# Output stage of a two-layer hybrid backbone: low halves and second gate factor to VectorE, retention rows and gate row loaded from GpSimd's queue

## The chip, the cores and the metric

The kernel runs on one core of one Trainium2 chip. Its metric is the device time in microseconds (us) of one execution. Before the change it was 3836.28 us, the median of three runs (3832.0 to 3844.18).

## The reference

Two layers are applied to a stream of 2048 latent tokens and 256 context tokens, each 1024 wide. One input projection feeds three groups of heads: latent attention (8 heads, 512 columns), retention (4 heads, 256 columns) and a convolution module (256 columns). Every group is multiplied by its own SiLU gate, the groups are joined, sent through one output projection, gated and normalised:

```
o_mla  = softmax(q k^T * scale) v  *  silu(pg_mla)
o_ret  = norm(retention forward + backward) * silu(pg_ret)
o_conv = conv_module(pglu) * silu(pg_conv)
y      = concat([o_mla, o_ret, o_conv]) @ w_out          # 1024 x 1024
x_new  = layer_norm(ALPHA * x + gate * y, ln_g, ln_b)
```

The context rows are needed in the first layer only; the second layer (`l == 1`, "layer 1" below) returns the 2048 latent rows.

## The kernel before, in words

Tokens are handled in units of 256 columns and tiles of 128 tokens (two tiles to a unit). Each layer has three stages: input projections, attention, output. The diff lies in the class `Output`, which does the last one. Its first generators already run beside the last quarter of attention's last head.

**What one unit needs.** `gen_prep` makes the left operand of the output projection. SyncE (its DMA queue is SP) loads the attention rows and the convolution rows of a unit into `ot` and the reciprocals of the softmax sums, spread over 64 partitions, into `rd`. GpSimd multiplies `ot` by `rd` (called P1 here; `ot<-ot,rd`, 128x1024). SP then loads the gate `gm_s` into the same `rd`, and the engine `W` multiplies again (P2, "the second gate factor"). For each of the two tiles ScalarE copies `ot` into the high half of `oh`, rounded to fp32r, and `W` subtracts to get the low half (`oh<-ot,oh`, once 128x256 and once 128x512). There are one `ot` and one `rd` tile, so the next unit's loads start only when the second tile's low halves have been taken, and four `oh` tiles. `W` is VectorE in layer 0 and GpSimd in layer 1 (line 1931).

**Retention.** `gen_rr` loads a tile's retention rows (`rr`, 384 KB) and a state block (`r_st`, 128 KB) from DRAM into one of two sets of buffers; `gen_ret`, in two lanes, scales on GpSimd (`qd<-rr,r_dq`, two per tile), transposes and multiplies on TensorE, masks, normalises and gates on VectorE and ScalarE, and writes columns 4 and 5 of `oh`. A set becomes free when TensorE's matmuls with `rr` are done.

**Projection and finish.** `run` goes through the tiles in order. Per tile TensorE does two groups of 24 matmuls (128x512, `bank<-wo,oh`) into three banks in turn; `post` on VectorE multiplies by the gate row `gb`, adds the residual `xo` and takes statistics; `gen_fin` normalises on ScalarE, applies `lnw` on GpSimd (two passes of 128x1024) and stores from GpSimd's queue. `gen_consts` loads `gb` first and sets `ready`, without which no `post` is written.

**What sets the order.** Every engine and SP works through its instructions in the order in which the program writes them. That order comes from a planner: each engine has a meter (`V`, `S`, `G`, `PE`, `SY`) that adds a cost for every instruction written (a DMA on GpSimd costs it 1000 ns), and a generator's `wait(...)` goes on when TensorE's meter has passed the named one. `wait(SY)` and a wait for a bare number, such as `wait(G.spent)`, add 2000 ns for a transfer; `wait(G)` adds 150 ns. So a changed engine changes what stands where in all queues.

Of the kernel before, what the change touches and what calls it, by code (L numbers as in the profile page):

```python
# [19 lines left out]
D = 1024  # L20
# [53 lines left out]
def tile_hybrid(ctx: ExitStack, tc: tile.TileContext, I: dict, out: bass.AP, stop: str = ""):  # L74
# [49 lines left out]
    V, S, G = Meter(nc.vector, v_cost), Meter(nc.scalar, s_cost), Meter(nc.gpsimd, g_cost)  # L124
    PE, SY = Meter(nc.tensor, p_cost), Meter(nc.sync, d_cost)
# [5 lines left out]
    def wait(*ms):  # L131
        at = max(m if isinstance(m, float) else m.spent for m in ms) + margin["engine"]
        if SY in ms or isinstance(ms[0], float):
            at += margin["dma"]
        yield
        while PE.spent < at:
            yield
# [1674 lines left out]
    class Output:  # L1812
# [101 lines left out]

        def gen_consts(self, ngb):
            l = self.l
            SY.dma_start(self.gb[:, 0, :], self.d["gate_s"][0:1, :].to_broadcast([128, D]))
            yield from wait(SY)
            self.ready = True
            SY.dma_start(self.lnw[:, 0, :], I["ln_g"][l:l + 1, :].to_broadcast([128, D]))  # L1920
            SY.dma_start(self.lnw[:, 1, :], I["ln_b"][l:l + 1, :].to_broadcast([128, D]))
            for j in range(1, ngb):
                SY.dma_start(self.gb[:, j, :], self.d["gate_s"][j:j + 1, :].to_broadcast([128, D]))

        def gens(self):
            l, d, last, tiles, att = self.l, self.d, self.last, self.tiles, self.att
# [1 line left out]
            OT, RD, XO, YO, RR, SS, GT = (self.OT, self.RD, self.XO, self.YO, self.RR,  # L1928
                                          self.SS, self.GT)
            OH, oh_of = self.OH, self.oh_of  # L1930
            W = G if last else V
            QP, KT, AM, QD, QT, YR = self.QP, self.KT, self.AM, self.QD, self.QT, self.YR
            gng, gnb = self.gng, self.gnb
            ohs, xs, rrs = {}, {}, {}
# [2 lines left out]
            def part(g):  # L1937
                parts[g] = parts.get(g, 0) + 1

            def gen_prep():  # L1940
                for g in self.units:
# [16 lines left out]
                    yield from wait(SY.spent + 1500.0, G.spent)  # L1958
                    W.tensor_tensor(ot[:, 0:4, :], ot[:, 0:4, :], rd, op=ALU.mult)
                    RD.put(rd)  # L1960
                    yield from wait(W)
                    for e in range(2):
# [6 lines left out]
                        yield  # L1969
                        W.after(S)  # L1970
                        W.tensor_tensor(oh[:, 1, 6:8, :], ot[:, 4:6, es], oh[:, 0, 6:8, :], op=ALU.subtract)
                        W.tensor_tensor(oh[:, 1, 0:4, :], ot[:, 0:4, es], oh[:, 0, 0:4, :], op=ALU.subtract)
                        if e == 1:
                            OT.put(ot)
                        yield from wait(W)
                        part(t)
# [109 lines left out]
            def gen_rr():  # L2086
                for t in tiles:
                    rr = yield from RR.grab()
                    ss = yield from SS.grab()
                    SY.dma_start(rr, d["ret_s"][t * 128:(t + 1) * 128, 0:768])  # L2090
                    SY.dma_start(ss, d["ss_s"][:, t, :])
                    yield from wait(SY)
                    rrs[t] = rr, ss

            def norm_gen(tiny, bs, n, tag, ps):
# [104 lines left out]
            def gen_fin(t, y, bs, ps):  # L2200
# [15 lines left out]
                YO.put(y)  # L2216

            self.gen_rr, self.gen_prep, self.gen_ret = gen_rr, gen_prep, gen_ret
            self.gen_x, self.gen_fin, self.gen_ctx = gen_x, gen_fin, gen_ctx

# [142 lines left out]
```

## Time and profile before

| | us |
|---|---|
| median of 3 runs | 3836.28 |
| the profiled execution | 3843.96 |
| its span, first to last instruction | 3842.2 |
| busy in the span: PE / DVE / ACT / POOL | 3637.0 / 2945.9 / 2222.8 / 2251.8 |
| share of the span: PE / DVE / ACT / POOL | 95% / 77% / 58% / 59% |
| first and last start of a matmul of the output projection in layer 1 | 3557.35 and 3827.4 |
| first matmul of it in layer 0 | 1652.0 |

PE is TensorE's matmuls, PEld its weight loads, DVE VectorE, ACT ScalarE, POOL GpSimd, SP SyncE's DMA queue. PE's busy time is modelled from matmuls that overlap, so 95% is not 95% of its peak. Nearly all instructions carry line L85, that of the meter that writes them, so groups are told apart by the names of their tiles.

### The profile page before, as it was taken

How to read it: one execution, taken by the hardware profiler on the slowest of the kernel's cores; microseconds unless marked ns; L12 is line 12 of the kernel's file. 1: busy time of each engine (PE TensorE's matmuls, PEld its weight loads, DVE VectorE, ACT ScalarE, POOL GpSimd, SP SyncE). 2: the span in 40 equal slices, each digit the busy share in tenths (PEclk: the TensorE clock that was granted, in tenths of full speed). 3: DMA queues.
4: the chain of work that ended last, by engine and by line, in shares of the span. 5: the costliest groups of instructions: out<-in, count | busy, mean ns of one | idle time of the engine just before them, and what ended most of it. 6: DMA issues, size and time to landing. Idle time of an engine off the chain costs nothing. (4 is left out here: it accounts for less than half of the span.)

```text
span 3842.2 us, 61498 instructions
## 1 busy us (share of the span) xinstructions
PE 3637.0 (95%) x21323; PEld 3078.9 (80%) x21323; DVE 2945.9 (77%) x6374; ACT 2222.8 (58%) x4248; POOL 2251.8 (59%) x1451
## 2 busy tenths in 40 slices
PE   7999999899999999989989999999999999999987
PEld 6999999877777777767768999998777777776776
DVE  4956847789988899858678568477898999998555
ACT  3433343178888888845344433431788888888332
POOL 0342333369998887724431523333699988887565
PEclk9999999999999999989989999999999999999998
DMA  5463646523323221155453746456222222211553
GB/s 194 143 208 106 197 129 190 166 64 84 91 71 81 68 58 29 46 144 164 146 194 102 223 116 199 131 186 169 55 57 71 64 59 46 48 30 40 165 155 99
DMA packets 415261, 440.69 MB, mean 115 GB/s; under 512 B 47915, under 2 KB 365981, under 8 KB 412773
## 3 DMA queue, kind: packets, MB, share of 16 engines
q1 hardware_dynamic: 410372, 420.25, 38.5%
q0 software_dynamic: 4576, 16.52, 1.1%
q8 instruction: 167, 2.74, 0.3%
q14 instruction: 146, 1.19, 0.1%
HBM read 295.99 MB, written 140.67 MB: 114 GB/s over the span
## 5 line engine op out<-in xcount | busy, mean ns | idle before, releaser
L85 POOL TENSOR_TENSOR acc<-acc,ph 128x1024 f32<-128x1024 f32 x448 | 1060.8, 2368 | 93.6 <-ACT ph L85 69.7
L85 PE MATMUL bank<-qt,kt 96*128 96x512 f32 (+1 forms) x3456 | 1004.0, 399 | 2.4 <-ACT qt L85 1.4
L85 DVE TENSOR_REDUCE mx<-bank 128x1 f32<-128x512 f32 (+1 forms) x1152 | 787.8, 686 | 144.8 <-PE bank L85 90.4
L85 PEld LDWEIGHTS bank<-qt,kt 96*128 96x128 f32 (+1 forms) x3456 | 653.8, 191 | 221.4 <-issue 16.9
L85 DVE TENSOR_TENSOR pl<-bank,ph 128x512 fp32r<-128x512 f32 x1152 | 783.6, 680 | 34.4 <-ACT ph L85 30.7
L85 ACT ACTIVATE bank<-bank 128x512 f32<-128x512 f32 (+2 forms) x1228 | 693.7, 565 | 180.7 <-DVE bank L85 108.8
L85 ACT CAST ph<-bank 128x512 fp32r<-128x512 f32 x1152 | 676.7, 587 | 67.7 <-POOL acc L85 5.4
L85 PE MATMUL bank<-w,u 128*128 128x256 f32 (+1 forms) x4224 | 550.4, 288 | 7.7 <-POOL w L85 4.8
L85 PE MATMUL bank<-u,w 128*128 128x256 f32 x4080 | 531.2, 288 | 12.4 <-ACT u L85 4.5
L85 PEld LDWEIGHTS bank<-w,u 128*128 128x128 f32 x4224 | 531.8, 191 | 10.8 <-POOL w L85 5.6
L85 PEld LDWEIGHTS bank<-u,w 128*128 128x128 f32 x4080 | 509.6, 193 | 19.0 <-ACT u L85 6.9
L85 POOL TENSOR_TENSOR w<-x,w 128x512 fp32r<-128x512 f32 (+2 forms) x214 | 266.9, 1266 | 367.6 <-ACT w L85 275.6
L85 PE MATMUL bank<-kt,qt 96*128 96x512 f32 (+1 forms) x1280 | 459.5, 378 | 13.1 <-DVE mx L85 10.4
L85 PE MATMUL bank<-ph,vt 128*128 128x512 f32 x1152 | 461.7, 401 | 9.4 <-ACT ph L85 7.8
L85 PE MATMUL bank<-wo,oh 128*128 128x512 f32 x1632 | 420.7, 412 | 39.1 <-POOL oh L85 18.8
L85 PE MATMUL bank<-pl,vt 128*65 128x512 f32 x1152 | 435.3, 396 | 3.9 <-DVE pl L85 3.2
L85 PEld LDWEIGHTS bank<-wo,oh 128*128 128x128 f32 x1632 | 312.1, 196 | 113.8 <-POOL oh L85 20.5
L85 DVE SCALAR_TENSOR_TENSOR bank<-wn,prmT,bank 128x384 f32<-128x384 f32 (+1 forms) x754 | 364.6, 565 | 0.0
L85 PEld LDWEIGHTS bank<-kt,qt 96*128 96x128 f32 x1280 | 243.3, 191 | 75.2 <-DVE mx L85 16.6
L85 POOL TENSOR_TENSOR t<-t,t 128x512 f32<-128x512 f32 x64 | 82.5, 1289 | 357.1 <-DVE t L85 314.4
L85 PEld LDWEIGHTS bank<-ph,vt 128*128 128x128 f32 x1152 | 217.1, 188 | 64.1 <-ACT o L85 12.8
L85 ACT CAST w<-x 128x512 fp32r<-128x512 f32 (+2 forms) x244 | 139.5, 606 | 203.3 <-DMA x<-in_w_in_dram 203.0
(267 smaller groups left out, 4313.7 us busy)
## 6 DMA issues: line engine op xcount, KB each, us to landing
x<-in_w_in_dram SPq DMA_DIRECT2D x110, 512.0 KB
q_s<-so SPq DMA_DIRECT2D x102, 256.0 KB
k_s<-so SPq DMA_DIRECT2D x72, 256.0 KB
v_s<-so SPq DMA_DIRECT2D x36, 512.0 KB
kt<-k_s SPq DMA_DIRECT2D x32, 576.0 KB
vt<-v_s SPq DMA_DIRECT2D x48, 384.0 KB
ret_s<-t SPq DMA_DIRECT2D x70, 256.0 KB
qt<-q_s SPq DMA_DIRECT2D x64, 256.0 KB
```

The lines of the kernel that those rows point to most:

```text
L85: return f(*a, **k)
```

## The change

`W` is VectorE in both layers, so that in layer 1 the second gate factor and the low halves from `ot` leave GpSimd. In both layers the retention rows, the state block and the first gate row are loaded from GpSimd's queue, not SP's, and the planner waits for GpSimd's meter plus a transfer. The rest of the loads (`gt`, `xo`, `ot`, `rd`, `lnw`) stay on SP.

```
 def gen_consts(self, ngb):
-    SY.dma_start(self.gb[:, 0, :], self.d["gate_s"][0:1, :].to_broadcast([128, D]))
-    yield from wait(SY)
+    G.dma_start(self.gb[:, 0, :], self.d["gate_s"][0:1, :].to_broadcast([128, D]))
+    yield from wait(G.spent)
     self.ready = True
...
-    W = G if last else V
+    W = V
...
 def gen_rr():
     for t in tiles:
         rr = yield from RR.grab()
         ss = yield from SS.grab()
-        SY.dma_start(rr, d["ret_s"][t * 128:(t + 1) * 128, 0:768])
-        SY.dma_start(ss, d["ss_s"][:, t, :])
-        yield from wait(SY)
+        G.dma_start(rr, d["ret_s"][t * 128:(t + 1) * 128, 0:768])
+        G.dma_start(ss, d["ss_s"][:, t, :])
+        yield from wait(G.spent)
         rrs[t] = rr, ss
```

## Rows read from the trace of the kernel before

**Rows 1.** Waits in layer 1's output stage: total us, times, longest.
```profile
PE bank L85 <- POOL oh L85: 18.8, 4, 6.2
POOL ot L85 <- DMA rd<-gm_s: 21.9, 6, 5.5
```

**Rows 2.** Timeline of PE there: start, length, instruction, idle before it and releaser.
```profile
3732.11 5.71 PE L85 MATMUL bank<-wo,oh 128*128 128x512 f32 x16 [6.23 <-POOL oh L85]
...
3744.34 5.74 PE L85 MATMUL bank<-wo,oh 128*128 128x512 f32 x24
...
3768.91 1.65 PE L85 MATMUL bank<-wo,oh 128*128 128x512 f32 x3 [5.32 <-POOL oh L85]
```

**Rows 3.** Stretches: length, PE busy (count), granted clock, DMA share, GB/s.
```profile
3732.00:3736.00 4.00, 3.89 (x9) 0.50 0.73 258
```

**Rows 4.** Timeline of POOL over one unit of layer 1.
```profile
3730.11 1.95 POOL L85 TENSOR_TENSOR oh<-ot,oh 128x256 fp32r<-128x256 f32 x2
...
3733.16 1.96 POOL L85 TENSOR_TENSOR oh<-ot,oh 128x256 fp32r<-128x256 f32 x2
3742.36 4.84 POOL L85 TENSOR_TENSOR wraw<-wraw,lnw 128x1024 f32<-128x1024 f32 x2 [7.24 <-ACT wraw L85]
...
3748.12 2.40 POOL L85 TENSOR_TENSOR ot<-ot,rd 128x1024 f32<-128x1024 f32 x1
...
3754.65 2.40 POOL L85 TENSOR_TENSOR ot<-ot,rd 128x1024 f32<-128x1024 f32 x1 [2.99 <-DMA rd<-gm_s]
3761.20 4.79 POOL L85 TENSOR_TENSOR yo<-yo,lnw 128x1024 f32<-128x1024 f32 x2 [4.14 <-ACT yo L85]
...
3766.90 1.96 POOL L85 TENSOR_TENSOR oh<-ot,oh 128x256 fp32r<-128x256 f32 x2
```

**Rows 5.** Timeline of POOL (its first row) and SP, 3695 to 3745.
```profile
3695.61 1.96 POOL L85 TENSOR_TENSOR oh<-ot,oh 128x256 fp32r<-128x256 f32 x2 [0.65 <-ACT oh L85]
3704.01 0.32 SPq L85 DMA_DIRECT2D rr<-ret_s  x1
...
3704.90 0.90 SPq L85 DMA_DIRECT2D ot<-o_s  x2
...
3744.34 0.34 SPq L85 DMA_DIRECT2D rr<-ret_s  x1
```

**Rows 6.** Groups in 3520 to 3842: count, busy us, mean ns, idle before.
```profile
L85 POOL TENSOR_TENSOR ot<-ot,rd 128x1024 f32<-128x1024 f32 x16 | 38.3, 2394 | 48.9 <-DMA rd<-rden_s 26.9 <-DMA rd<-gm_s 21.9
L85 POOL TENSOR_TENSOR oh<-ot,oh 128x512 fp32r<-128x512 f32 x16 | 21.2, 1327 | 0.0
L85 POOL TENSOR_TENSOR oh<-ot,oh 128x256 fp32r<-128x256 f32 x16 | 11.7, 730 | 5.9 <-ACT oh L85 5.8
```

**Rows 7.** Groups of VectorE in layer 0's output stage, 1640 to 1962.
```profile
L85 DVE TENSOR_TENSOR oh<-ot,oh 128x512 fp32r<-128x512 f32 x17 | 20.3, 1197 | 0.1
L85 DVE TENSOR_TENSOR ot<-ot,rd 128x1024 f32<-128x1024 f32 x8 | 12.9, 1612 | 10.9 <-DMA rd<-gm_s 10.9
L85 DVE TENSOR_TENSOR oh<-ot,oh 128x256 fp32r<-128x256 f32 x17 | 12.7, 750 | 6.7 <-PE bank L85 4.7 <-ACT oh L85 2.0
```

**Rows 8.** Timeline of VectorE in layer 0: second gate factor and low halves.
```profile
1891.49 1.64 DVE L85 TENSOR_TENSOR ot<-ot,rd 128x1024 f32<-128x1024 f32 x1 [6.32 <-DMA rd<-gm_s]
...
1941.18 2.28 DVE L85 TENSOR_TENSOR ot<-ot,rd 128x1024 f32<-128x1024 f32 x1 [1.05 <-DMA rd<-gm_s]
1946.44 1.01 DVE L85 TENSOR_TENSOR oh<-ot,oh 128x256 fp32r<-128x256 f32 x2
```

**Rows 9.** Timeline of PE in layer 0's output stage.
```profile
1679.29 1.12 PE L85 MATMUL bank<-identr,rr 128*128 128x128 f32 x4 [3.07 <-DMA rr<-ret_s]
...
1893.52 6.75 PE L85 MATMUL bank<-wo,oh 128*128 128x512 f32 x16 [6.60 <-DVE oh L85]
```

**Rows 10.** Waits of SP in layer 1's output stage: total us, times, longest.
```profile
SPq L85 <- PE bank L85: 92.5, 19, 10.5
```

**Rows 11.** Stretch of layer 1: length; PE, PEld, DVE, ACT, POOL busy (count); clock; DMA; GB/s.
```profile
3690.00:3830.00 140.00, 119.00 (x562) 97.42 (x560) 74.62 (x236) 42.62 (x111) 78.36 (x60) 0.93 0.40 121
```

## The prediction

> **What bounds the kernel now.** I read the page's busy table first: TensorE is busy 95% of the span, so a change to other engines can only pay where TensorE stands still. The code then says where to look: `W` changes in layer 1 only, the loads in both layers. Next I read layer 1's output stage by stretches. From 3690 to 3830 us TensorE is busy 119.0 of 140.0 us at a granted clock of 0.93, GpSimd 78.4, VectorE 74.6 [rows 11]: nobody is full, so something waits in a chain. The view of waits names it: TensorE waited 18.8 us in four pieces for `oh` from GpSimd [rows 1], that is, for the low halves that the change moves. The timeline of TensorE shows two of the four, 6.23 and 5.32 us, one per unit [rows 2].
>
> A stall costs more than its length. In 3732 to 3736 us the granted clock is 0.50, the lower of the two levels (1.2 GHz), right after 6.23 us in which TensorE did nothing [rows 3]. 16 matmuls then took 5.71 us, while 24 took 5.74 us a little later [rows 2]: 0.357 against 0.239 us each, or 1.9 us lost. For four stalls I take 4 x 1.9 = 7.6 us. So 18.8 + 7.6 = 26.4 us can be had here at most.
>
> Why the low halves come late is in GpSimd's timeline over one unit [rows 4]. From the first tile's low halves (3730.11) to the next unit's (3766.90) are 36.8 us: 5.0 to the end of the second tile's low halves (3735.12), 13.0 to P1 (loads into the one `ot` and `rd`, then GpSimd's finishing passes and store), 6.5 to P2 (P1 and the gate's load), 12.25 from P2 to the low halves. In the last piece GpSimd works 2.40 on P2, then waits 4.14 for ScalarE's `yo`, spends 4.79 on the finish of another tile and 0.9 on its store, with the low halves queued behind all that. TensorE needs less for a unit: from 3732.11 until it ran dry at 3768.91 - 5.32 = 3763.59 are 31.5 us, 29.6 without the 1.9 of the low clock [rows 2]. The stage thus goes at the pace of this chain, 36.8 against 29.6, and 36.8 - 29.6 = 7.2 is the stall plus its low clock.
>
> **The change part by part.** *P2 and low halves to VectorE, layer 1.* GpSimd loses 8 of the 16 products (19.2 us) and both kinds of low halves (21.2 + 11.7), 52.1 us [rows 6]. VectorE gets them. Layer 0 already does them there: 1.612, 1.197 and 0.750 us each [rows 7], so 8 x 1.612 + 16 x (1.197 + 0.750) = 44.1 us, about 22 of them in the stretch of [rows 11], where VectorE then has some 97 of 140: room enough. What counts is the chain. Its last piece is now P2 on VectorE, ScalarE's copies, low halves on VectorE. Layer 0 has that from 1941.18 to 1946.44, 5.3 us [rows 8], against 12.25. I leave the other pieces as they are: the low halves cost about the same (1.95 on either engine), and the loads do not change. The chain is then 5.0 + 13.0 + 6.5 + 5.3 = 29.8 us.
>
> *Retention rows and state block to GpSimd's queue.* Two loads per tile. A store from GpSimd takes it 0.9: the finishing passes end at 3765.99, and what stands behind their store starts at 3766.90 [rows 4]. At 0.9 each that is 3.6 us per unit. I put half of it ahead of P1: 1.8 us; between 0 (all of it in the 7.24 us that GpSimd waits for ScalarE) and 3.6. Chain: 31.6 us, 2.0 more than TensorE's 29.6.
>
> The new wait is the buffer's: a load of `rr` must wait for TensorE's matmuls of an earlier tile. SP stood there 92.5 us in 19 waits, 10.5 at the longest [rows 10]. On GpSimd the instructions behind it are `qd`, P1 and the finishing passes; P1 is on the chain. The nearest rows speak for a short wait: SP sent one `rr` at 3744.34 [rows 5], when GpSimd was in the midst of finishing passes (3742.36 to 3747.20) that it had itself waited for [rows 4], so it would hardly have come to the load sooner. I take 0 on top of the 1.8, with 2 x 4.9 (92.5/19, two tiles per unit) as the dear end.
>
> SP is rid of those waits. In one unit it matters by the rows: the second tile's low halves ended at 3697.57, but the loads of `ot` went out at 3704.90, after `rr` at 3704.01 [rows 5]: 7.3 us lost in the queue. I take this as gone; otherwise that unit keeps its stall. What is late next on SP is `xo`, which waits for VectorE.
>
> The Trainium skill speaks against this step: "DMA: Bandwidth & Descriptors", section "Issuing engines are not separate DMA queues", says that starting transfers from several engines saves only the time a sequencer needs to start them. By that rule the move would give back some 0.9 us of the 7.3 and the gain below would be 12.0 instead of 18.4; the row shows SP held by a buffer rather than by issue time, so I go by the row and keep the rule as a rival.
>
> *Gate row to GpSimd's queue, and the loads in layer 0.* `W` stays VectorE in layer 0, so only the queue changes there. At the entry to that stage one TensorE wait hangs on an `rr` load, 3.07 us [rows 9]; the gate row is loaded in the same place of each stage. The largest stall, 6.60 us, follows VectorE's wait for the second gate [rows 8, 9], which these loads do not touch. I count 0 for both, between 3.1 gained (the entry wait gone) and 3.1 lost (as much again).
>
> *Sum.* 26.4 to be had, less 2.0 for each of four units, 8.0: 18.4 us. Against the profiled execution's 3843.96 that is 3825.6; that execution was 7.7 us above the median of the runs, and taken from the median, 3836.28, the forecast is 3818 us.
>
> **The rivals.**
> (a) *VectorE takes over the wait for the gate.* P2 waits for `rd<-gm_s`; on GpSimd that was 21.9 us in six waits [rows 1] and held only finishing work. On VectorE the retention mask, `post` and the retention's low halves stand behind it, and TensorE waits for those. Layer 0 shows it: P2 waited 6.32 us and TensorE then 6.60 [rows 8, 9]. Against it: in another unit there the wait was 1.05. If 13 of the 21.9 us reach TensorE, 18.4 - 13 = 5.4 is left: 3831 us.
> (b) *The queue move saves only issue time*, the mechanism named with the rule above: SP is then held by `xo` where `rr` held it, one unit keeps 7.3 - 0.9 = 6.4 us, and the gain is 12.0: 3824 us.
> (c) *Slower: GpSimd is held by the retention buffer.* If the loads of `rr` are written ahead of P1 and GpSimd comes to them early, the chain grows by up to 2 x 4.9 to 41.4 us, 4.6 above the old 36.8; over four units 18 us more: 3855 us. It decides from 36.8 - 31.6 = 5.2 us of such waiting per unit on. For it: GpSimd loses 52.1 us of work and adds about 30 of issues (33 loads at 0.9), so it comes earlier. Against it: GpSimd mostly stands in a finishing pass when the buffer gets free.
> (d) *The change does not do what it says*: the new costs reorder what the planner writes, and other work moves in between P2 and the low halves as the finishing passes did. No gain: 3836 us.
>
> **How the numbers follow.** Forecast 0.58, (a) 0.20, (b) 0.08, (c) 0.10, (d) 0.04. A measurement of this kernel can tell about 0.3%, 11.5 us, from no change. Faster by more: nearly all of the forecast, half of (b) and a little of (a), 0.63. Within: most of (a), half of (b), (d) and the forecast's edge, 0.26. Slower by more: (c), 0.11. The forecast's own range is 3806 (all 26.4, and a few us from the entry and layer 0) to 3826 (3.6 instead of 1.8 us of issues ahead of P1 and a slow clock behind the stalls that are left). To hold the time 8 times in 10 it goes up over (a) to 3838; (c) is left out, and a little below 3806.
>
> **What would show it.** Right: `PE <- POOL oh` is gone from layer 1; units there follow each other in about 30 to 32 us; VectorE's low halves start about 5 us after P2; the granted clock of the late stretches is nearer to 1.00; GpSimd's busy time falls by about 52 us. The issues: 0.9 us each on GpSimd, in its idle time. Wrong: TensorE's waits for VectorE's `oh` or `am` grow by over 10 us behind waits of VectorE for `rd<-gm_s` (a); loads of `ot` still leave SP many us after the low halves (b); GpSimd idle for TensorE ahead of `rr` with P1 behind it (c); TensorE's gaps in layer 0 grow.

## The result and the profile after

The change makes the kernel slower: 3875.08 us, the median of 4 runs (3866.03 to 3884.42), against 3834.14 us for the kernel before on the same chip. The ratio is 1.0108, with a 95% interval of 1.0091 to 1.0125, so 41 us are lost. The forecast, 3818 us with a range of 3806 to 3838, was wrong in sign; what happened is rival (c), to which it gave 0.10.

First the waits of layer 1's output stage, 3510 to 3883 us (what waits, for what: us in total, times, the longest):

```profile
POOL rr L85 <- PE bank L85: 108.1, 12, 16.4
...
PE bank L85 <- DVE am L85: 24.8, 7, 4.3
...
DVE ot L85 <- DMA rd<-gm_s: 19.1, 6, 3.5
```

The stall that the prediction set out to remove, TensorE waiting for `oh` from GpSimd (18.8 us in [rows 1]), has gone. Another one stands in its place: 24.8 us for `am`, the masked retention product of VectorE. And SP's wait for the retention buffer [rows 10] has moved to GpSimd with the loads: 108.1 us in 12 waits, 9.0 each, against 4.9 each on SP.

The timelines of one unit tie the two together (start, length, instruction, and in brackets the idle time before it and what ended it). GpSimd:

```profile
3675.44 1.21 POOL L85 TENSOR_TENSOR qd<-rr,r_dq 128x256 f32<-128x256 f32 x2
3691.11 0.58 POOL L85 DMA_DIRECT2D rr<-ret_s  x1 [14.45 <-PE bank L85]
3691.68 0.54 POOL L85 DMA_DIRECT2D r_st<-ss_s  x1
3692.24 4.89 POOL L85 TENSOR_TENSOR yo<-yo,lnw 128x1024 f32<-128x1024 f32 x2
3697.42 0.58 POOL L85 DMA_DIRECT2D out_dram<-yo  x1 [0.30 <-POOL yo L85]
3698.02 2.40 POOL L85 TENSOR_TENSOR ot<-ot,rd 128x1024 f32<-128x1024 f32 x1
...
3704.13 5.64 POOL L85 TENSOR_TENSOR yo<-yo,lnw 128x1024 f32<-128x1024 f32 x2 [2.55 <-ACT yo L85]
...
3711.76 0.55 POOL L85 DMA_DIRECT2D rr<-ret_s  x1 [1.09 <-PE bank L85]
```

SP, which sends the loads for P1 and, behind P1, the gate's load:

```profile
3678.83 0.97 SPq L85 DMA_DIRECT2D ot<-o_s  x2
3679.85 1.25 SPq L85 DMA_DIRECT2D rd<-rden_s  x2
3700.46 0.36 SPq L85 DMA_DIRECT2D rd<-gm_s  x1
```

VectorE:

```profile
3704.30 3.25 DVE L85 TENSOR_TENSOR ot<-ot,rd 128x1024 f32<-128x1024 f32 x1 [3.00 <-DMA rd<-gm_s]
3707.47 0.68 DVE L85 TENSOR_TENSOR am<-bank,r_dm 128x512 f32<-128x512 f32 x1
```

TensorE, the first four of five stalls of this kind that follow each other:

```profile
3670.79 0.69 PE L85 MATMUL bank<-rr,am 128*128 128x64 f32 x2 [4.31 <-DVE am L85]
...
3708.20 0.69 PE L85 MATMUL bank<-rr,am 128*128 128x64 f32 x2 [4.31 <-DVE am L85]
...
3745.60 0.67 PE L85 MATMUL bank<-rr,am 128*128 128x64 f32 x2 [4.31 <-DVE am L85]
...
3783.14 0.66 PE L85 MATMUL bank<-rr,am 128*128 128x64 f32 x2 [4.31 <-DVE am L85]
```

Read in order of time: GpSimd stands 14.45 us at the load of `rr`, until TensorE has done its last matmul with that buffer. Behind the load stand a finishing pass and its store, and only then P1, at 3698.02. P1's own operands are not what is late: their loads left SP some 17 us before, and P1's row shows no wait for them. SP can send the gate's load only when P1 has read `rd`, at 3700.46. VectorE stands 3.00 us for that load with P2, P2 takes 3.25, and `am` is queued behind it. TensorE stands still for 4.31. The matmuls that follow free the buffer for the next load, which GpSimd sends at 3711.76, right behind them. So the pattern locks: 37.4 us from stall to stall (3745.60 - 3708.20), against 36.8 for the old chain.

The stall again costs more than its length. These are stretches of the kernel after; the columns are those of [rows 11]:

```profile
3690.00:3830.00 140.00, 122.77 (x574) 102.93 (x574) 97.82 (x264) 44.44 (x119) 72.97 (x58) 0.90 0.43 136
3704.00:3708.00 4.00, 0.00 (x0) 0.00 (x0) 3.70 (x2) 0.76 (x3) 3.80 (x2) 1.00 0.28 107
3708.00:3710.00 2.00, 1.80 (x9) 1.80 (x9) 2.00 (x3) 1.29 (x4) 1.76 (x1) 0.53 0.00 0
...
3712.00:3714.00 2.00, 2.00 (x6) 1.52 (x6) 1.79 (x11) 0.10 (x1) 1.99 (x4) 0.50 0.64 199
```

After 4.31 us in which TensorE did nothing, the granted clock is 0.50 to 0.53 (1.2 GHz, the lower level). Over the 140 us it is 0.90, below the 0.93 of [rows 11]. VectorE has gone from 74.62 to 97.82 us busy, the 97 that the prediction worked out, so it is not full; what it does is late.

Where the 41 us lie is read from the first and last start of the output projection's matmuls. First the kernel before, then the kernel after (layer 0, layer 1):

```profile
L85 PE MATMUL bank<-wo,oh x864: 387/394/795, 1652.0 to 1978.6; 128*128 128x512 f32 x173
L85 PE MATMUL bank<-wo,oh x768: 387/395/795, 3557.3 to 3827.4; 128*128 128x512 f32 x192
```

```profile
L85 PE MATMUL bank<-wo,oh x864: 387/394/796, 1651.2 to 1991.6; 128*128 128x512 f32 x173
L85 PE MATMUL bank<-wo,oh x768: 387/395/797, 3574.7 to 3862.4; 128*128 128x512 f32 x192
```

Layer 0's stage ends 13.0 us later. Attention carries that shift along (its first matmul in layer 1 starts at 2692.6 instead of 2679.7) and its end adds 4.4 (3574.7 - 3557.3 = 17.4). Layer 1's stage is 287.7 us instead of 270.1, so 17.6 longer. The rest, 5.5 us, lies behind the last matmul, where the two programs do the same work (the last section comes back to it).

### The profile page after: what moved, and what is told of

It is laid out like the page before. It is cut to its first block, busy times and chain, and to the rows that moved or that the text cites. A ratio compares the mean times of both kernels' runs of the same rounds, so it can differ in the third digit from the quotient of the medians.

```text
span 3882.7 us, 61473 instructions
## 1 busy us (share of the span) xinstructions
PE 3655.2 (94%) x21323; PEld 3096.2 (80%) x21323; DVE 2985.8 (77%) x6414; ACT 2214.5 (57%) x4244; POOL 2249.5 (58%) x1481
## 5 line engine op out<-in xcount | busy, mean ns | idle before, releaser
L85 PEld LDWEIGHTS bank<-wo,oh 128*128 128x128 f32 x1632 | 318.0, 200 | 98.1 <-DVE oh L85 15.5
L85 POOL TENSOR_TENSOR acc<-ph 128x1024 f32<-128x1024 f32 x64 | 151.4, 2366 | 177.5 <-ACT ph L85 176.6
```

The lines of the kernel that those rows point to most:

```text
L85: return f(*a, **k)
```

## The experiments

Theory T: GpSimd, held by the loads of `rr`, comes late to P1; the gate's load and P2 come late behind it, and P2 holds `am` on VectorE. Rival R: moving P2 to VectorE is itself the harm. Twelve kernels were run. "Ratio" is the time over that of the kernel before on the same chip, with its 95% interval.

| kernel | median us | ratio |
|---|---|---|
| the whole change | 3875.08 | 1.0108 (1.0091 to 1.0125) |
| `W` only (e1) | 3823.38 | 0.9971 (0.9955 to 0.9987) |
| retention loads only (e2) | 3846.09 | 1.0032 (1.0019 to 1.0046) |
| gate row only (e7) | 3788.92 | 0.9900 (0.9886 to 0.9915) |
| without the gate row (e3) | 3857.64 | 1.0079 (1.0064 to 1.0094) |
| without the retention loads (e9) | 3808.41 | 0.9938 (0.9917 to 0.9958) |

Not all kernels ran on the same chip, so they are compared by their ratios. The length of a stage comes from one profiled execution of a kernel, while the runs of one kernel spread over 4 us (e8) to 25 us (e1): a few us between two stages tell nothing.

### One part at a time: e1 and e2

e1 is the kernel before with `W = V`.

> Only the compute half of the change: second gate product and low halves of layer 1 on VectorE, all loads as in the kernel before. Theory T (the loads on GpSimd's queue did the harm: GpSimd, held 14 to 16 us by the retention buffer, comes late to the first gate product, so the gate load and the second product come late): without them the gain forecast for this half alone shows, 3810 to 3830 us, TensorE's stall for `oh` from GpSimd is gone and no stall of 4.3 us for `am` is left at every unit. Rival R (the second product on VectorE itself holds `am` and stalls TensorE): 3850 to 3865 us, with the stalls for `am` of some 4 us per unit still there. Layer 0 is as before under both.

e2 is the kernel before with only this edit:

```
-                    SY.dma_start(rr, d["ret_s"][t * 128:(t + 1) * 128, 0:768])
-                    SY.dma_start(ss, d["ss_s"][:, t, :])
-                    yield from wait(SY)
+                    G.dma_start(rr, d["ret_s"][t * 128:(t + 1) * 128, 0:768])
+                    G.dma_start(ss, d["ss_s"][:, t, :])
+                    yield from wait(G.spent)
```

> Only the retention rows and state blocks move to GpSimd's queue, in both layers; second product and low halves of layer 1 stay on GpSimd, gate row on SP. T: GpSimd stands for TensorE's release of `rr` in both layers and now has the low halves queued behind that as well: slower than before, 3855 to 3885 us, with layer 0's output stage some 10 us longer. R: no change, 3822 to 3846 us.

e1 came out at 3823.38 us, e2 at 3846.09. R is out as the cause of the 41 us: the compute half alone is a gain, and the waits of e1 in layer 1 show it without the loss:

```profile
DVE ot L85 <- DMA rd<-gm_s: 15.5, 5, 5.4
...
PE bank L85 <- DVE am L85: 3.0, 5, 0.8
```

VectorE waits for the gate's load there too, 15.5 us, but TensorE's wait for `am` is 3.0 us and not 24.8. Two P1 of e1 are 31.6 us apart (3682.28 and 3713.91), against the 37.4 of the whole change. e2 is slower, clear of no change by its interval, but it lies at R's upper edge (3846) and 9 us below T's lower one: GpSimd stood 61.9 us for the buffer, not 108.1; there it still had the low halves to do. Some 5 of the 12 us lie at the program's end (last section), and layer 0, which T expected some 10 us longer, ends at 1976.2, 2 earlier than before. Worth noting is that the parts do not add: -11 and +12 us by the ratios, while both together with the gate row left on SP (e3) give +30.

### Fewer holds: e4 and e5

e4 is the whole change with a third set of buffers in layer 1; e5 writes the loads later.

```
+            if self.last:
+                self.RR.put(p.tile([128, 768], F32, name="rr2"))
+                self.SS.put(p.tile([128, 256], F32, name="ss2"))
```

> The whole change, with a third buffer for the retention rows and for the state block in layer 1 (layer 0 has no room for it and stays as changed). T: GpSimd's holds for TensorE in layer 1 fall from 108 us to under 40, the first gate product comes earlier, the stalls for `am` shrink, and some 15 to 22 us come back: 3848 to 3862 us against 3875 of the whole change. R: the holds go but the time stays, 3867 to 3883 us.

```
                     ss = yield from SS.grab()
+                    yield from wait(PE.spent + 2000.0)
                     G.dma_start(rr, d["ret_s"][t * 128:(t + 1) * 128, 0:768])
```

> The whole change, but the loads of the retention rows are written 2 us (of the planner's time) later, behind the point where TensorE is through with the buffer, in both layers. T: GpSimd's holds shrink in both layers, part of the time comes back: 3835 to 3862 us; what is left depends on how late the rows then land. R: no gain, 3867 to 3885 us, with TensorE's waits for `rr` longer.

e4 came out at 3863.19 us (ratio 1.0078, 1.0060 to 1.0097). Its holds fell only to 60.4 us in 7 waits, and TensorE's waits for `am` to 9.2. T had asked for under 40 us of holds and 3862 us at most, R for 3867 at least; the gain has T's sign, but the interval touches that of the whole change, so by itself e4 settles little. e5 came out at 3814.65 us (0.9946, 0.9926 to 0.9965), better than T's own range: in layer 1's waits GpSimd does not wait for TensorE at `rr` any more, and layer 0's last output matmul starts at 1965.5 us, 13 before that of the kernel before. By the intervals e5 is level with e9 below (0.9938), which has the same loads on SP: written behind the release, they cost nothing on GpSimd's queue that these runs can tell, though the order of the rest differs too.

### The planner's order or the hold: e14

In both e4 and e5 the order of all work differs from the whole change's. e14 keeps it: on TensorE, VectorE, ScalarE and GpSimd the instructions stand as in the whole change, only the retention loads are sent by SP.

```
-                    G.dma_start(rr, d["ret_s"][t * 128:(t + 1) * 128, 0:768])
-                    G.dma_start(ss, d["ss_s"][:, t, :])
+                    nc.sync.dma_start(rr, d["ret_s"][t * 128:(t + 1) * 128, 0:768])
+                    nc.sync.dma_start(ss, d["ss_s"][:, t, :])
+                    G.spent += 2000.0
```

> The whole change in its own order of instructions on every compute engine, with the retention loads booked on GpSimd by the planner but sent by SP. Theory T (GpSimd, standing for TensorE's release of the buffer, is what makes the change slow): the holds go to SP, the stalls for `am` go or shrink, and most of the loss comes back: 3790 to 3835 us. Rival O2 (the order that the planner writes for the whole change is what makes it slow): 3860 us or more, with the same stalls.

It came out at 3835.60 us (1.0012, 0.9998 to 1.0025), 0.6 above T's slow edge: by the ratios 37 of the 41 us are back, some 5 of them at the program's end (last section). The waits of layer 1, SP's first:

```profile
SPq L2090 <- PE bank L85: 95.5, 14, 14.0
```

```profile
DVE ot L85 <- DMA rd<-gm_s: 8.8, 5, 1.9
...
PE bank L85 <- DVE am L85: 6.8, 8, 2.9
```

The wait for the buffer is as long as before, 95.5 us, but now SP does the waiting. VectorE's wait for the gate falls from 19.1 to 8.8 us and TensorE's for `am` from 24.8 to 6.8. Layer 1's stage takes 256.3 us (3559.5 to 3815.8) in place of 287.7. Layer 0 ends at 1987.5 us, only 4 earlier than in the whole change. So most of the 13 us lost there do not need a GpSimd that is held. That they come from the order that the planner writes is likely but not shown, for in e14 SP takes over the holds in layer 0 too (98.6 us in 14 waits), and VectorE's wait for the gate, whose load SP sends, grows from 18.6 to 31.6 us.

### The last link: e6, and with it e8 and e10

If T is right, the holds hurt only through the gate's load. In e6 the whole change stays and layer 1 gets a tile of its own for the second gate factor, loaded beside the first:

```
+            self.GM = Slots([])
+            if self.last:
+                self.GM.put(p.tile([128, 4, UN], F32, name="gm"))
...
+                    gm = rd
+                    if last:
+                        gm = yield from self.GM.grab()
+                        SY.dma_start(gm, d["gm_s"][:, ts].rearrange("(k p) t -> p k t", p=128))
                     yield from wait(SY)
                     G.tensor_tensor(ot[:, 0:4, :], ot[:, 0:4, :], rd, op=ALU.mult)
-                    SY.dma_start(rd, d["gm_s"][:, ts].rearrange("(k p) t -> p k t", p=128))
+                    if not last:
+                        SY.dma_start(rd, d["gm_s"][:, ts].rearrange("(k p) t -> p k t", p=128))
...
-                    W.tensor_tensor(ot[:, 0:4, :], ot[:, 0:4, :], rd, op=ALU.mult)
+                    W.tensor_tensor(ot[:, 0:4, :], ot[:, 0:4, :], gm, op=ALU.mult)
```

> The whole change, and in layer 1 the second gate factor gets a tile of its own, loaded together with the first one, so that VectorE no longer waits for it behind the first product. GpSimd is held by the retention buffer as before. Theory T: the hold still delays the first product, but the 3.7 us of load and some 2.4 of queueing between the two products go; the stalls of 4.3 us for `am` shrink to under 1.5 and 15 to 25 us come back: 3850 to 3860 us. Rival H (the hold itself sets the period, the load between the products does not matter): units keep 37 us each, 3868 to 3880 us, with the stall moved to another wait of TensorE.

It came out at 3831.62 us (1.0007, 0.9996 to 1.0018), 18 us below T's range. Its waits in layer 1:

```profile
POOL rr L85 <- PE bank L85: 83.2, 9, 16.5
...
PE bank L85 <- DVE am L85: 1.2, 6, 0.4
```

And a stretch of it (length; PE, PEld, DVE, ACT, POOL busy; clock):

```profile
3690.00:3790.00 100.00, 97.76 (x500) 79.88 (x499) 85.91 (x225) 37.42 (x104) 52.21 (x43) 1.00 0.55 163
```

GpSimd still stands 83.2 us for the buffer, up to 16.5 at a time, and in this stage it no longer matters: TensorE is busy 97.76 of 100 us at the full clock, and two P1 are 31.1 us apart (3675.21 and 3706.29), not H's 37. Another order is hardly the reason: counted in the traces, GpSimd's list differs from the whole change's in 5 of 1377 places, TensorE's in 98 of 21323. So in layer 1 the hold by itself is not the price; the price is what stood behind it in series, P1, the gate's load and P2 ahead of `am`. Layer 0, which has no such tile here, still ends at 1989.1 us.

The same tile added to e1 is e8:

> The compute half alone (3823 us) with the same own tile for the second gate factor in layer 1. T: without held loads VectorE's 15.5 us of waits for that load cost TensorE little, so 0 to 8 us are gained: 3815 to 3823 us. Rival (the wait for the load is what keeps the compute half from its 18 us): 3805 to 3813 us.

It came out at 3808.33 us (0.9953, 0.9937 to 0.9970), in the range of the rival: the wait for the gate's load is what kept the compute half from its 18 us. By the ratios that half is worth 11 us without the tile and 18 with it; the intervals overlap, so for this pair the reading is likely rather than shown. The pair of e9 and e10 below shows such a cost clear of noise.

### The gate row: e3 and e7

e3 is the whole change with the first gate row back on SP, e7 the kernel before with only that row on GpSimd's queue:

```
-            SY.dma_start(self.gb[:, 0, :], self.d["gate_s"][0:1, :].to_broadcast([128, D]))
-            yield from wait(SY)
+            G.dma_start(self.gb[:, 0, :], self.d["gate_s"][0:1, :].to_broadcast([128, D]))
+            yield from wait(G.spent)
```

> The whole change with the gate row back on SP's queue. It asks where the 13 us that the whole change loses in layer 0's output stage come from, since the retention loads alone lost none there (last output matmul of layer 0 at 1976.2 us, before 1978.6, whole change 1991.6). Theory G (the gate row behind a held GpSimd, 16 us at the entry): without it that matmul is back at 1976 to 1980 us, layer 1 keeps its stalls for `am`, and the time is 3855 to 3865 us. Rival P (the retention loads, by another order of the work): 1988 to 1993 us and 3868 to 3880 us.

> Only the gate row moves to GpSimd's queue; all else as before the change. Nothing holds GpSimd for TensorE, so theory G expects no change, 3822 to 3846 us, and the row some us earlier than on SP, with layer 0's last output matmul at 1972 to 1980 us. Rival (the row itself is harmful on that queue): 3845 us or more.

e3 came out at 3857.64 us with layer 0's last output matmul at 1976.3 and 22.0 us of TensorE's waits for `am` in layer 1, the numbers of theory G. Its mechanism does not hold, though: in e14 nothing holds GpSimd ahead of the gate row, and layer 0 still ends at 1987.5, so the wait ahead of the row is not needed for the loss. What is left is the row's place in the planner's order, which no run tests by itself here. e7 fell outside both expectations: 3788.92 us, 40 below the kernel before. One transfer per layer, moved to another queue, is the best of the whole change. Layer 1 of e7:

```profile
3630.00:3750.00 120.00, 120.00 (x631) 101.28 (x630) 77.58 (x259) 48.06 (x129) 88.14 (x65) 1.00 0.54 169
```

TensorE is busy throughout, at the full clock. `W` is still GpSimd there, and its timeline shows why the stall for `oh` has gone all the same:

```profile
3681.17 2.39 POOL L85 TENSOR_TENSOR ot<-ot,rd 128x1024 f32<-128x1024 f32 x1 [2.99 <-DMA rd<-gm_s]
3683.53 2.07 POOL L85 TENSOR_TENSOR oh<-ot,oh 128x256 fp32r<-128x256 f32 x2
3685.92 4.86 POOL L85 TENSOR_TENSOR yo<-yo,lnw 128x1024 f32<-128x1024 f32 x2 [0.33 <-ACT yo L85]
...
3711.07 2.39 POOL L85 TENSOR_TENSOR ot<-ot,rd 128x1024 f32<-128x1024 f32 x1 [3.10 <-DMA rd<-gm_s]
3713.42 2.05 POOL L85 TENSOR_TENSOR oh<-ot,oh 128x256 fp32r<-128x256 f32 x2
```

The first low halves follow P2 at once and the finishing pass comes after them; in [rows 4] it stood ahead of them, with GpSimd's wait for ScalarE. The period is 29.9 us (3711.07 - 3681.17), TensorE's own pace.

Is it the queue or the order? e13 has e7's order on every engine, while SP sends the row:

```
-            SY.dma_start(self.gb[:, 0, :], self.d["gate_s"][0:1, :].to_broadcast([128, D]))
-            yield from wait(SY)
+            nc.sync.dma_start(self.gb[:, 0, :], self.d["gate_s"][0:1, :].to_broadcast([128, D]))
+            G.spent += 1000.0
+            yield from wait(G.spent)
```

> The gate row alone gained 40 us (3789). Here the kernel before gets the same order of instructions on every engine as that one, because the planner books the gate row's cost on GpSimd, but the transfer itself is sent by SP, at the same place of the program. Theory O (the gain comes from the other order that the planner writes; the queue that carries the row hardly matters): 3785 to 3800 us. Rival Q (the gain comes from the row's leaving SP's queue): 3818 us or more.

It came out at 3796.87 us (0.9910, 0.9892 to 0.9927). So 36 of the 40 us come from the planner's booking the row on another meter; the queue itself is worth at most the small rest, which the intervals do not tell from nothing.

### The change without its retention loads: e9 and e10

> The change without its retention loads: gate row on GpSimd's queue, second product and low halves of layer 1 on VectorE, retention loads on SP. If the two parts added up as measured alone (-40 and -8.5 us): 3780 us. T with a TensorE-bound layer 1 (the gate row's order has already removed the stall for `oh`, so the second part has little left to gain): 3780 to 3795 us. Rival (VectorE's wait for the gate load spoils the new order): 3800 us or more.

> As the run without the retention loads, with a tile of its own for the second gate factor in layer 1. If VectorE's wait for that load costs something there, some 5 to 15 us below that run; if TensorE already sets the pace of layer 1 (about 30 us for a unit), within 5 us of it.

e9 came out at 3808.41 us (0.9938), the expectation of its rival: with the order that the gate row brings, moving `W` to VectorE costs about 15 us more than it brings (layer 1's stage takes 252.8 us, from 3537.1 to 3789.9, against e7's 243.2), as there was no stall left to remove. In this order R's harm is real, though smaller than the 41 us. e10, with the gate's own tile, came out at 3790.84 us (0.9893, 0.9876 to 0.9910), level with e7 and 17.6 below e9 on the same chip, a little more than the 15 expected at most: VectorE's wait for the gate's load is what e9 paid for.

e10 is also e6 with the retention loads back on SP, and between these two are 44 us by the ratios. Layer 1's stage accounts for little of it (244.0 against 250.5 us), layer 0 for most: there e10 ends at 1960.6, e6 at 1989.1. So the own tile cures the stalls of layer 1, not all that the retention loads cost on GpSimd's queue with the order that they bring; what costs it in layer 0 stays open. The fastest version found is thus e7, or e10, and both beat the kernel before by about 1%.

## Why the prediction was wrong

**What bounds the kernel: right.** The stall for `oh` was GpSimd's chain, and e7 shows the ceiling: without it TensorE is never idle over 120 us of layer 1, and that stage is 26.9 us shorter (243.2 against 270.1), where 26.4 had been worked out.

**P2 and low halves to VectorE: right, for this part alone.** 18.4 us were forecast (with all of SP's relief counted in). e1 gained 11 (5 to 17) and e8, where rival (a)'s wait is taken away, 18 (11 to 24). That units of e1 take the 31.6 us of the forecast is luck: 1.8 of those were for loads on GpSimd's queue, which e1 leaves on SP; without them the chain was put at 29.8. In the order of e9 the same part is a loss.

**The step that failed** is the retention loads: "I take 0 on top of the 1.8, with 2 x 4.9 as the dear end". The row that spoke for 0 was [rows 4 and 5]: GpSimd was in the midst of finishing passes when SP got the buffer. But that row is of a GpSimd that had 52 us more to do. The change takes that work away, so GpSimd reaches the load early and stands there, 9.0 us on average, or 18 us for the two loads of a unit, and 14.45 at one load of the unit shown. The document's own rival (c) says so ("GpSimd loses 52.1 us of work ... so it comes earlier") and puts the point from which it decides at 5.2 us per unit; it was passed by far. A row of the kernel before was used for an engine whose load the change itself had altered. Of the 57 us between forecast and result, e14 gives 37 to the queue of these loads (some 5 of them at the program's end); the other 20 are there with SP as the sender too, and their cause is in part open (layer 0, below).

**Two rivals were one chain.** (a) and (c) were weighed apart. (a)'s condition, that VectorE gets to the gate's load before it has landed, is what (c) brings about: a late P1 makes a late load. Together they give the 24.8 us for `am`; e6, which cuts (a)'s link and leaves (c)'s holds in place, takes these stalls away (1.2 us left) and brings the time back to that of the kernel before. (c)'s own place was off by one engine, for it expected TensorE to wait for `oh` on a long chain, and 3855 us was too little by 20.

**Issue time: too dear.** 0.9 us each were taken from a store; the loads took GpSimd 0.58 and 0.54. The store too takes 0.58, behind 0.30 of waiting for the pass ahead of it.

**Layer 0 and the gate row: counted 0, and wrong.** The bounds of 3.1 us had been taken from one entry wait. Layer 0 lost 13 us, and the row alone moves the time by 40. The 40 are nearly all an effect of the planner's order (e13); for the 13 it is likely, and no run shows it. Rival (d) had the order at 0.04 and with the wrong size, since it allowed the order only to cancel the gain.

**Rival (b)** does not hold. With the same order on every compute engine, the sender of the loads alone decided over 37 us (e14). The Trainium skill, "DMA: Bandwidth & Descriptors", section "Issuing engines are not separate DMA queues", lets the starting engine matter only by the time to start a transfer. For the gate row the runs fit that: e13 and e7 differ only in its sender, and their intervals overlap. For the retention loads they do not, for there the starting engine also waits for the buffer, with work queued behind it.

## What to carry to other kernels

A load that must wait for a buffer belongs on a queue behind which nothing urgent stands; on a compute engine's queue it is a wait of that engine, and the freer the engine, the longer it stands (here 61.9 us with the low halves on GpSimd, 108.1 without). Before you take a wait's length from a trace, ask whether the change itself alters the load of the engine that will do the waiting. And where a planner writes the order, an edit's booked cost is an edit too: compare a run that has the new order and the old queue with one that has both.

## Not expected of the hardware

*The end of the program.* Behind the last store SP waits for TensorE's sequencer before the program closes. First e2, then the kernel before (SP's waits at the end):

```profile
SPq L2359 <- PEq L2359: 7.1, 2, 6.4
```

```profile
SPq L2359 <- PEq L2359: 1.7, 2, 1.3
```

The longer wait is 6.4 or 6.5 us in every kernel whose retention loads go out from GpSimd (the whole change and e2 to e6), and 1.2 or 1.3 in the others, e7 with its gate rows on GpSimd and e14 among them. So the loads cost some 5.2 us there, part of the 41; what is done in that time stays open.

*Two engines on one product.* P2 on VectorE took 2.84 us on average in the whole change (8 instructions), 1.47 in e1 and 1.59 in e6. In the timeline above its 3.25 us lie beside a finishing pass of GpSimd that took 5.64 us for two instructions, which take 4.8 to 4.9 elsewhere. The Trainium skill, "SBUF — State Buffer", section "SBUF: two separate sides", says that a VectorE operation with two SBUF inputs and a GpSimd operation that reads SBUF exclude each other for whole instructions. The trace agrees in that both are longer when they meet; that one stands still while the other works is not read from these rows. In the locked pattern they met in most units: six of GpSimd's pairs of passes in that stage took 5.6 us.
